# A second level of Strassen products for one more of the seven products in a tuned MLP kernel: four operand sums, results in tiles of their own, some differences on GpSimd

## The chip, the cores and the metric

The kernel runs on one core of one Trainium2 chip. The metric is device time in microseconds (us) for one execution; a lower time is better. The mean granted TensorE clock was 1.00 in the kernel before.

Names of engines as in the profile: PE is TensorE (matmuls), PEld its weight loads, DVE is VectorE, ACT is ScalarE, POOL is GpSimd, SP is the engine that issues most DMA loads (SPq is its sequencer).

## The reference

```python
x = randn(8, 1024, 1024); w1 = randn(1024, 4096); w2 = randn(4096, 1024)   # float32
h = x @ w1
h = 0.5 * h * (1 + tanh(sqrt(2 / pi) * (h + 0.044715 * h ** 3)))
return (h @ w2).astype(float32)
```

## The kernel before

The 8192 rows are handled as eight blocks of 1024 (0 to 7). In each block, M1 is `x @ w1` with the activation, and M2 is the product with `w2`. Both use Strassen's seven products instead of eight, with half-precision operands. In M2 some of those seven products are split once more, each into seven smaller ones (here called a *split* product; the others are *plain*). A plain product of M2 is 64 matmuls of 512 columns, a split one is 7 x 16 = 112 matmuls of 256 columns.

Blocks 0 and 1 make the weight sums and write them to DRAM (no split products). Block 2 splits products 6 and 7 and meanwhile makes the split weights of 1 and 3. Blocks 3 to 7, the *late blocks*, split 1, 3, 6 and 7. The order of products in M2 is 4, 1, 2, 3, 5, 6, 7.

One shared pool of 26 big tiles, `up` (4 KB in each of 128 partitions, shown as `u` in the profile), holds M1's weights, all weight tiles of M2, the operands made by VectorE, the next block's transposed x, and results on their way to DRAM.

```python
    up = ctx.enter_context(tc.tile_pool(name="up", bufs=26))
    gcp = ctx.enter_context(tc.tile_pool(name="gcp", bufs=4))      # operand sums, "gc"
    tp = ctx.enter_context(tc.tile_pool(name="tp", bufs=10))       # small temporaries, "tmp", 2 KB
    # ...
    class Inner:                                  # one split product
        def load(self):
            for j in ORDER:                       # seven weight tiles of 512 KB, issued by SP
                self.y[j] = unit(NI // 2, OH // 2)          # unit() takes a tile of `up`
                nc.sync.dma_start(out=self.y[j], in_=in_d[self.m][:, j - 1])
        def make_x(self, b): ...                  # one difference of g, VectorE, a tile of `up`
        def make(self, j): ...                    # one operand sum, VectorE, a tile of `gcp`; five per product
        def steps(self):
            # ...
            pb, qb, rb = psum(), psum(), psum()
            self.multiply(4, pb, True)            # 16 matmuls each
            v = temp()
            nc.scalar.copy(out=v, in_=pb)
            yield 4                               # fill-in work for VectorE stands at the yields
            self.multiply(5, qb, True)
            u = tile(results, 0)
            tt(u, v, qb, SUB, True)
            # ... 1, 2, 3, 7, 6: results go on in PSUM (pb, qb, rb), are added into acc,
            #     or leave through two result tiles
    # ...
    def matmul2(sb, g, next_x):
        # ...
        order = (4, 1, 2, 3, 5, 6, 7)
        load(4)
        run((0, 0))
        for m, after in zip(order, order[1:] + (None,)):
            if after is not None:
                load({1: 2, 2: 3, 3: 5}.get(m, after))     # loads of the next product
            if m == (1 if sb == 2 else 3):
                at["xs"] = next_x()               # 16 transposing loads, SP, four tiles of `up`
            if m in inner:
                for j in products[m].steps():
                    run((m, j))
                continue
            # ... a plain product; product 2 goes on in the PSUM banks of product 4
```

## Time and profile before

| | before |
|---|---|
| median of the first runs | 1542.41 us |
| PE busy | 1530.6 us of a span of 1541.5 |
| VectorE, ScalarE, GpSimd busy | 1072.1, 504.4, 278.1 us |
| DMA | 395.8 MB, mean 257 GB/s |

The head of the profile page, and its part 4, the chain of waits by engine:

```profile
PE 1530.6 (99%) x8318; PEld 814.8 (53%) x8318; DVE 1072.1 (70%) x1332; ACT 504.4 (33%) x852; POOL 278.1 (18%) x386
...
PE 94%; DMA 4%; DVE 1%; issue 0%; ACT 0%; SPq 0%; POOL 0%; DVEq 0%; POOLq 0%
```

The chain in order of time, for the M2 of block 4 and the M1 behind it. Columns: start (us), length (us), what; L757 are plain products, L675 split ones, L368 is M1:

```profile
884.97 13.81 PE ps L757 x64
898.79 12.23 PE ps L675 x112
911.01 13.81 PE ps L757 x64
924.83 12.23 PE ps L675 x112
937.05 13.81 PE ps L757 x64
950.87 24.45 PE ps L675 x224
975.32 96.69 PE ps L368 x448
```

There is no gap between the pieces: PE never waits here. A plain product takes 13.81 us and a split one 12.23 us, so splitting one more is worth 1.58 us.

SP's loads in the same M2, from its timeline (start, length of the run of issues, line, what, how many). The block's M2 starts at 884.97:

```profile
883.28 2.13 SPq L271 DMA_DIRECT2D u<-raw_d  x4
885.46 15.42 SPq L660 DMA_DIRECT2D u<-in_d  x7
904.06 3.81 SPq L271 DMA_DIRECT2D u<-raw_d  x4
908.05 21.92 SPq L352 DMA_TRANSPOSE u<-xb  x16
930.07 29.98 SPq L660 DMA_DIRECT2D u<-in_d  x14
```

These are the loads of products 2, 3, 5, the x of the next block, and products 6 and 7 (14 tiles). The first tile of product 6 is issued at 930, 21 us before PE needs it at 950.9. SP itself waits here for stores of results to land and free a tile, as its list of waits for this M2 shows:

```profile
SPq L660 <- DMA out_dram<-u: 20.7, 2, 13.2
```

PE does not feel these two waits, because the loads are still early enough.

### The profile page before, as it was taken

What the parts mean: (1) busy time and instruction counts of PE and PEld (TensorE: products, weight loads), DVE (VectorE), ACT (ScalarE), POOL (GpSimd) and SP (SyncE); (2) the same over time, 40 slices, a digit from 0 to 9 for tenths busy, and PEclk for the clock granted to TensorE, in tenths of its full rate; (3) what the DMA queues carried; (4) which work ended last, traced back from release to release, by engine and by line L of the source; (5) the groups of instructions that cost most, each with busy time, mean ns of one, the idle gap of its engine ahead of it and who ended that gap; (6) DMA issues with size and microseconds to landing.
All of it is one profiled execution on the core that took longest, in us unless ns stands there. A gap on an engine that the chain in (4) does not pass through costs nothing.

```text
span 1541.5 us, 22131 instructions
## 1 busy us (share of the span) xinstructions
PE 1530.6 (99%) x8318; PEld 814.8 (53%) x8318; DVE 1072.1 (70%) x1332; ACT 504.4 (33%) x852; POOL 278.1 (18%) x386
## 2 busy tenths in 40 slices
PE   9999999999999999999999999999999999999998
PEld 4444444444444447445664457544675447744466
DVE  5876867758755677557865578656786566955676
ACT  6655024410244112442134411344114431144311
POOL 1242011112201042001320013200141001400023
PEclk9999999999999999999999999999999999999999
DMA  9999875884985799957898589975799669994577
GB/s 310 346 329 348 250 272 188 282 254 148 349 271 161 195 369 315 310 150 236 259 321 291 135 251 293 331 234 175 221 315 326 193 182 257 304 342 131 187 251 192
DMA packets 211980, 395.76 MB, mean 257 GB/s; under 512 B 77344, under 2 KB 95776, under 8 KB 210976
## 3 DMA queue, kind: packets, MB, share of 16 engines
q1 hardware_dynamic: 175968, 297.86, 59.0%
q0 software_dynamic: 35904, 96.49, 23.0%
q8 instruction: 65, 1.06, 0.3%
q14 instruction: 43, 0.35, 0.1%
HBM read 294.65 MB, written 114.29 MB: 265 GB/s over the span
## 4 chain that ended last, share of the span: by engine, by line
PE 94%; DMA 4%; DVE 1%; issue 0%; ACT 0%; SPq 0%; POOL 0%; DVEq 0%; POOLq 0%
PE ps L368 49%; PE ps L757 29%; PE ps L675 16%; DMA u<-in_d 1%; DMA gc<-in_w_dram 1%; DMA u<-w_d 1%; DMA out_dram<-u 1%; DMA in_d<-u 1%; DVE u L150 0%; DVE tmp L150 0%; SPq L160 0%; ACT u L219 0%; POOL out_dram L466 0%; ACT g L378 0%; ACT u L323 0%
## 5 line engine op out<-in xcount | busy, mean ns | idle before, releaser
L368 PE MATMUL ps<-u 128*128 128x512 f16 x3584 | 776.3, 379 | 4.8 <-DVE tmp L150 1.9
L150 DVE TENSOR_TENSOR tmp<-tmp,ps 128x512 f32<-128x512 f32 x546 | 374.2, 687 | 309.2 <-ACT tmp L430 113.0
L368 PEld LDWEIGHTS <-u 128*128 128x128 f16 x3584 | 350.3, 98 | 428.5 <-issue 4.6
L757 PE MATMUL ps<-u,gc 128*128 128x512 f16 x1472 | 320.3, 379 | 0.0
L378 ACT ACTIVATE g<-tmp 128x512 f16<-128x512 f32 x256 | 161.2, 630 | 295.2 <-DVE tmp L150 295.1
L757 PEld LDWEIGHTS <-gc 128*128 128x128 f16 x1472 | 144.0, 98 | 171.6
L150 DVE TENSOR_TENSOR u<-u 128x2048 f16<-128x2048 f16 (+3 forms) x194 | 186.4, 989 | 28.6 <-ACT u L323 12.5
L675 PE MATMUL ps<-u,gc 128*128 128x256 f16 x1760 | 198.3, 273 | 0.0
L675 PEld LDWEIGHTS <-gc 128*128 128x128 f16 x1760 | 172.2, 98 | 19.9
L378 ACT ACTIVATE g<-ps 128x512 f16<-128x512 f32 x256 | 151.5, 596 | 89.8 <-PE ps L368 89.7
L757 PE MATMUL ps<-u,g 128*128 128x512 f16 x704 | 153.7, 379 | 0.0
L150 DVE TENSOR_TENSOR u<-u,ps 128x512 f32<-128x512 f32 x124 | 84.7, 683 | 51.9 <-PE ps L675 16.4
L150 DVE TENSOR_TENSOR gc<-g,g 128x2048 f16<-128x2048 f16 x92 | 113.8, 1244 | 3.0 <-PE ps L757 1.6
L757 PEld LDWEIGHTS <-g 128*128 128x128 f16 x704 | 68.9, 98 | 83.0
L474 POOL DMA_DIRECT2D out_dram<-u x84 | 81.9, 1105 | 132.7 <-ACT u L696 123.6
L150 DVE TENSOR_TENSOR gc<-u 128x2048 f16<-128x2048 f16 x85 | 102.3, 1219 | 0.0
L813 ACT COPY tmp<-ps 128x512 f32<-128x512 f32 x52 | 30.5, 586 | 196.2 <-PE ps L757 172.6
L150 DVE TENSOR_TENSOR tmp<-ps,tmp 128x512 f32<-128x512 f32 x128 | 88.4, 690 | 5.9 <-PE ps L368 1.2
L466 POOL DMA_DIRECT2D out_dram<-tmp x76 | 53.7, 712 | 212.0 <-ACT tmp L813 110.3
L430 ACT COPY tmp<-ps 128x512 f32<-128x512 f32 x128 | 72.9, 570 | 49.3 <-PE ps L368 36.0
L150 DVE TENSOR_TENSOR u<-g,g 128x2048 f16<-128x2048 f16 x68 | 80.2, 1220 | 3.5 <-ACT g L378 3.5
L713 POOL TENSOR_TENSOR u<-u,tmp 128x512 f32<-128x512 f32 x12 | 20.6, 1721 | 292.0 <-DVE tmp L150 288.3
(40 smaller groups left out, 501.1 us busy)
## 6 DMA issues: line engine op xcount, KB each, us to landing
u<-in_d SPq DMA_DIRECT2D x154, 512.0 KB, 6.2
u<-w_d SPq DMA_DIRECT2D x240, 256.0 KB, 5.4
u<-raw_d SPq DMA_DIRECT2D x80, 512.0 KB, 6.3
out_dram<-u POOLq DMA_DIRECT2D x116, 256.0 KB, 8.5
gc<-in_w_dram SPq DMA_DIRECT2D x48, 512.0 KB, 6.0
u<-raw_d SPq DMA_DIRECT2D x96, 256.0 KB, 5.7
out_dram<-tmp POOLq DMA_DIRECT2D x76, 256.0 KB, 5.5
raw_d<-u SPq DMA_DIRECT2D x32, 512.0 KB, 9.5
```

Source lines behind the costliest of these rows:

```text
L150: i = nc.vector.tensor_tensor(out=out, in0=in0, in1=in1, op=op)
L368: nc.tensor.matmul(bank, lhsT=ops[:, k, :], rhs=xs[m][:, k, :], start=(first and k == 0), stop=(k == KH - 1), skip_group_check=not first,)
L378: gelu_last[0] = nc.scalar.activation(out=g[b][:, c, :], in_=src, func=GELU)
L430: nc.scalar.copy(out=v, in_=pb)
L466: return nc.gpsimd.dma_start(out=out2[r0:r0 + P, o0:o0 + OH], in_=src, **kw)
L474: return queue.dma_start(out=rows, in_=src, **(dict(accum_op=ADD) if add else {}))
L675: nc.tensor.matmul(bank[:, i * OH // 2:(i + 1) * OH // 2], lhsT=t[:, c, i * P:(i + 1) * P], rhs=self.y[j][:, c, :], start=(first and i == ...
L713: nc.gpsimd.tensor_tensor(out=quarter(acc, b), in0=quarter(acc, b), in1=pair(t), op=ADD)
L757: nc.tensor.matmul(bank, lhsT=a[:, c, :], rhs=pieces[c // QC][:, c % QC, :], start=(first and c == 0), stop=(c == NI - 1), skip_group_chec ...
L813: nc.scalar.copy(out=t, in_=ps)
```

## The change

Its intent: split product 2 as well, so 28 split products instead of 22. To pay for the additional VectorE work, every split product uses a form with four operand sums on each side instead of five (four sums of g and four sums of weights), and gathers its four quarters in result tiles of its own; product 4's block is stored and product 2's quarters are added to it in DRAM. Half of the differences of g for products 1 and 2 are made by GpSimd during M1. The split weights of product 2 are made in block 1. Cut to its core:

```diff
-INNER = (6, 7, 1, 3)
-ORDER = (4, 5, 1, 2, 3, 7, 6)
+MADE_INNER = (6, 7)
+FROM_2 = (2,)
+INNER = MADE_INNER + FROM_2 + (1, 3)
+S_TERMS = {1: "11", 2: "12", 4: "22"}
+S_SUMS = {1: (5, "21", ADD, "22"), 2: (6, 1, SUB, "11"), 3: (7, "11", SUB, "21"), 4: (3, "12", SUB, 2)}
+EARLY = ((1, "11"), (1, "21"), (2, "11"), (2, "21"))
+W_ORDER = (1, 6, 2, 7, 5, 4, 3)
...
-    dict(inner=(1, 3, 6, 7), fill=fills(
-        s00="x122 x112 x111 x121 a15 a11 a12 a17", ...
+    dict(inner=(1, 2, 3, 6, 7), fill=slots("""00:x122 x112 a11 a12 a13 a14 x222 x212
+    ;12:a21;14:a22;15:a23;17:a24
+    ;21:u0 u1;22:a31;23:u2 u3;24:a32;25:a33 d11;26:d22;27:a34 d21 d12
+    ;32:g50;34:g51 e11;35:g52 e22;36:e21;37:g53 e12""" ...
-    dict(inner=(6, 7), ...                       # block 2
+    dict(inner=(2, 6, 7), ...
...
+            if sb > 1 and c >= NI - 4:            # M1, GpSimd
+                m, b = EARLY[c - NI + 4]
+                if m in FILL_2[sb == 2]["inner"]:
+                    early[m][b] = unit(NI // 2, HT // 2)
+                    gu, gv = (inner_block(g[t], b) for t in A_TERMS[m])
+                    nc.gpsimd.tensor_tensor(out=early[m][b], in0=gu, in1=gv, op=SUB)
...
+        def steps(self, into):                    # into: two tiles of `up`
+            ab, bb, cb = psum(), psum(), psum()
+            self.multiply(1, ab, True)
+            v = temp()
+            nc.scalar.copy(out=v, in_=ab)
+            yield 1
+            self.multiply(6, bb, True)
+            tt(c12, pair(v), pair(bb), ADD, True)
+            yield 2
+            self.multiply(2, ab, False)
+            nc.scalar.copy(out=c11, in_=pair(ab))
+            self.done("11", c11)
+            yield 3
+            self.multiply(7, bb, False)
+            tt(c21, pair(v), pair(bb), ADD, True)
+            # ... 5, 4, 3
...
         def post4(q, ps):
             nc.scalar.copy(out=u[q], in_=ps)
+            store(sb, "21", q, u[q])              # product 2's quarters are added to this in DRAM
...
-                load({1: 2, 2: 3, 3: 5}.get(m, after))
+                load(after)
```

The last two lines ask for the loads in the same order in both kernels; the change there is one of form.

## The prediction

> **What bounds the kernel now.** The matmul stream. PE has 94% of the chain of waits, which is almost one unbroken PE chain from 63 us to 1537.5 us; the list of waits has PE waiting under 8 us in all. The granted clock was 1.00. The time is start-up (some 60 us, untouched), the matmul pieces, and a 4 us tail.
>
> In the chain in order of time, a plain M2 product (64 matmuls of 512 columns) takes 13.81 us; one split at the second level (112 matmuls of 256 columns) takes 12.23 us; M1 takes 96.69 us per block. So weight loads (98 ns each) still hide behind a 109 ns half-width matmul, and a split is worth 1.58 us.
>
> **Removed, added, moved.**
> - PE: product 2 becomes split in all six late blocks. The other splits keep 112 matmuls in another order. 6 x 1.58 = 9.5 us less, all on the critical path. Matmuls of 256 columns go from 2464 to 3136.
> - VectorE, per late block: 128x2048 half-precision differences 45 -> 41 (1.22 us each, 1.14 us apart), 128x512 fp32 additions in M2 34 -> 41 (0.69 us, 0.60 us apart). About even: some 70 us of work in the 75 us after product 4. Counting VectorE by hand against PE, I find it 2 to 4 us behind after products 2 and 3, and nothing late for PE.
> - ScalarE: 24 -> 18 copies of 0.59 us. Not critical.
> - GpSimd: 12 fp32 additions (128x512, 1.27 to 2.18 us) go; 22 differences of 128x2048 come in the last four chunks of M1, by my estimate 4 x 1.27 = 5 us each. The Trainium skill ("SBUF - State Buffer", Who interferes with whom) says that a VectorE operation with two SBUF inputs and a GpSimd operation that reads SBUF block each other; the trace fits (beside a 2.18 us GpSimd addition a VectorE difference took 1.70 instead of 1.22 us). In M1 one VectorE input is PSUM, so only the last difference should collide with VectorE's first of M2. Hidden.
> - DMA: per late block 7 instead of 4 weight tiles of 0.5 MB (+1.6 MB), and product 4's "21" block is stored, then added to (+1 MB). DMA share is about 0.93 over M2, 1.0 to 1.1 in products 6, 7 and early M1, but 0.48 late in M1, and loads are issued two products ahead. This is the main risk: perhaps 5 to 9 us more DMA work per block, and 26 buffers cap the look-ahead. I expect 0 to 0.5 us of PE waiting per block.
> - Block 1 splits product 2's weights while VectorE idles 7.5 us in product 4: free.
>
> **Predicted.** 1542.4 - 9.5 + about 1.5 of new waits = 1534.5 us, 8 in 10 between 1530 and 1544. Faster by over 2%: 0.01; within 2%: 0.96; slower by over 2%: 0.03.
>
> **What would show it.** Right: late M2 sections in the chain of 88.8 us instead of 90.4; PE idle under 10 us in the list of waits; VectorE busy within 1% of 1072 us; GpSimd busy up by 70 to 100 us; DMA moving 20 to 25 MB more. Wrong: PE waiting for weight tiles of products 2, 3 or 6, or for VectorE in products 3 or 6.
>
> **What would make it wrong.** Loads starved of buffers (the four early tiles hold them during M1), adding stores holding up the GpSimd queue and thereby buffers, or VectorE lagging over 5 us, which stalls PE on a PSUM bank.

## More of the kernel before

All runs that are compared here are of the fast state.

Part 6 of the page, the group of split weights (kilobytes each, median us from issue to landing):

```profile
u<-in_d SPq DMA_DIRECT2D x154, 512.0 KB, 6.2
```

## The result, and the profile after

The changed kernel takes 1579.24 us (median of 4 runs), the kernel before 1543.62 us in the same rounds: ratio 1.023, with a 95% interval of 1.0206 to 1.0253. It is correct and slower. Ratios here are the mean time of one kernel's fast runs over that of the other's fast runs of the same rounds, so they are not quite the ratio of the medians quoted.

The same views of the changed kernel. The head of the page and the chain of waits by engine:

```profile
PE 1531.9 (97%) x8606; PEld 839.5 (53%) x8606; DVE 1066.9 (68%) x1354; ACT 486.2 (31%) x821; POOL 387.2 (25%) x434
...
PE 75%; DMA 14%; DVE 4%; issue 4%; SPq 1%; ACT 1%; POOL 1%; POOLq 0%; DVEq 0%
```

PE has 75% of the chain instead of 94%. PE's list of waits (engine, line, what it waited for: us in total, times, longest), first the longest entry before, then the top of the list after:

```profile
PE ps L368 <- DVE tmp L150: 1.9, 2, 1.4
```

```profile
PE ps L686 <- DVE u L146: 11.9, 5, 10.3
PE ps L686 <- DMA u<-in_d: 11.8, 11, 2.0
PE ps L686 <- ACT tmp L704: 4.3, 6, 0.7
PE ps L686 <- DVE gc L146: 3.3, 6, 1.4
PE ps L364 <- DMA u<-w_d: 3.3, 9, 0.5
```

SP's timeline in block 4; M2 starts at 901.67 here:

```profile
887.19 35.80 SPq L668 DMA_DIRECT2D u<-in_d  x21
929.00 3.95 SPq L267 DMA_DIRECT2D u<-raw_d  x4
933.12 26.81 SPq L348 DMA_TRANSPOSE u<-xb  x16
960.03 18.34 SPq L668 DMA_DIRECT2D u<-in_d  x14
```

The loads of products 6 and 7 start at 960.0, which is 58 us into M2 instead of 45, and only 8 us before PE needs the first of them at 968.06. PE's timeline there, with the waits in brackets:

```profile
971.56 1.91 PE L686 MATMUL ps<-u 128*128 128x256 f16 x16
975.42 1.92 PE L686 MATMUL ps<-u,gc 128*128 128x256 f16 x16 [1.96 <-DMA u<-in_d]
978.04 1.38 PE L686 MATMUL ps<-u 128*128 128x256 f16 x11 [0.70 <-DMA u<-in_d]
...
991.99 3.65 PE L686 MATMUL ps<-u,gc 128*128 128x256 f16 x32 [1.07 <-DMA u<-in_d]
```

The loads also take longer from issue to landing, by part 6 of the page (6.2 us before):

```profile
u<-in_d SPq DMA_DIRECT2D x196, 512.0 KB, 7.8
```

From the landing times in the traces, counted after 700 us: mean 6.2 and 90th percentile 9.1 us before, 8.8 and 17.3 us after.

Block 2 shows a second kind of wait. VectorE's timeline, then PE's:

```profile
595.85 2.36 DVE L146 TENSOR_TENSOR u<-g,g 128x2048 f16<-128x2048 f16 x2 [11.15 <-DMA out_dram<-u]
```

```profile
598.27 3.53 PE L686 MATMUL ps<-u 128*128 128x256 f16 x16 [10.29 <-DVE u L146]
```

VectorE waits 11.15 us to write a new difference into a tile, because a store of results out of that tile has not landed. These differences are PE's own operand: the second of them ends at 598.21 and PE's matmuls start at 598.27, after waiting 10.29 us. (With 28 tiles, in experiment 12, it is the emptying of PSUM, queued on VectorE behind such a difference, that PE waits for.)

**Where the time went.** To add it up I took, from each trace, the distance between the starts of successive matmuls less the regular spacing (215.8 ns for 512 columns, 109.2 ns for 256), and summed what was over 60 ns. In us, one profiled run each:

```
              M2 of block 2   M2 of blocks 3-7   M1 of blocks 3-7
before              0.7              0.0                1.0
after              16.5             27.3                6.0
```

The change lost 49.8 us of PE time from block 2 on where before lost 1.7. That is 48 us of new waiting against the 9.5 us gained; with some 1 us less in the start-up it agrees with the measured difference of the two spans, 1578.6 - 1541.5 = 37.1 us.

**A third thing in the trace: the order of PE's work.** The order of instructions in the built programs (it is fixed when the kernel is compiled) shows that the scheduler moved PE's matmul groups. In block 3, written with the product (1, 2) and the part:

```
program order:  1.1 1.6 1.2 1.7 1.5 1.4 1.3 | 2.1 2.6 2.2 2.7 2.5 2.4 2.3
emitted, after: 1.1 1.6 1.2 1.5 2.1 2.2 1.4(2) 1.7 1.4(14) 2.6(6) 1.3 2.6(10) 2.5 ...   (n): n of 16 matmuls
```

Part 2.2 stands straight behind 2.1 and adds to the same PSUM bank, which ScalarE must copy first: those are the waits for `ACT tmp L704`. It should also hold the weight tiles of two products for longer; that was not measured.

### The profile page after: what moved, and what is told of

It reads as the page before. It is cut to its first block, busy times and chain, and to the rows that moved or that the text cites. A ratio compares the mean times of both kernels' runs of the same rounds, so it can differ in the third digit from the quotient of the medians.

```text
span 1578.6 us, 22771 instructions
## 1 busy us (share of the span) xinstructions
PE 1531.9 (97%) x8606; PEld 839.5 (53%) x8606; DVE 1066.9 (68%) x1354; ACT 486.2 (31%) x821; POOL 387.2 (25%) x434
## 4 chain that ended last, share of the span: by engine, by line
PE 75%; DMA 14%; DVE 4%; issue 4%; SPq 1%; ACT 1%; POOL 1%; POOLq 0%; DVEq 0%
PE ps L364 46%; PE ps L749 20%; PE ps L686 9%; DMA u<-in_d 6%; DMA u<-w_d 3%; DMA out_dram<-u 3%; DVE u L146 3%; DMA gc<-in_w_dram 2%; DVE gc L146 1%; DMA in_d<-u 1%; SPq L156 1%; DMA out_dram<-tmp 1%; ACT u L803 0%; SPq L348 0%; POOL u L159 0%
## 5 line engine op out<-in xcount | busy, mean ns | idle before, releaser
L364 PEld LDWEIGHTS <-u 128*128 128x128 f16 x3584 | 349.1, 98 | 433.8 <-DMA u<-w_d 8.5
L749 PE MATMUL ps<-u,gc 128*128 128x512 f16 x1088 | 237.4, 380 | 0.0
L146 DVE TENSOR_TENSOR u<-u 128x2048 f16<-128x2048 f16 (+3 forms) x245 | 219.0, 923 | 18.2 <-ACT u L319 12.2
L686 PEld LDWEIGHTS <-gc 128*128 128x128 f16 x1792 | 174.1, 98 | 36.8 <-issue 9.0
L749 PEld LDWEIGHTS <-gc 128*128 128x128 f16 x1088 | 106.4, 98 | 126.3
L477 POOL DMA_DIRECT2D out_dram<-u x108 | 111.5, 1033 | 246.6 <-DVE u L146 183.2
L460 POOL TENSOR_TENSOR u<-g,g 128x2048 f16<-128x2048 f16 x22 | 89.1, 4072 | 296.9 <-ACT g L374 296.9
L686 PE MATMUL ps<-u 128*128 128x256 f16 x1104 | 136.4, 275 | 23.4 <-DVE u L146 11.2
L686 PEld LDWEIGHTS <-u 128*128 128x128 f16 x1104 | 107.8, 98 | 43.8 <-DVE u L146 17.0
L146 DVE TENSOR_TENSOR u<-tmp,ps 128x512 f32<-128x512 f32 x56 | 38.4, 686 | 109.4 <-PE ps L686 72.0
L146 DVE TENSOR_TENSOR u<-g,g 128x2048 f16<-128x2048 f16 x70 | 83.5, 1220 | 19.6 <-DMA out_dram<-u 11.1
L427 ACT COPY tmp<-ps 128x512 f32<-128x512 f32 x128 | 72.9, 569 | 73.8 <-PE ps L364 73.6
L146 DVE TENSOR_TENSOR gc<-g,g 128x2048 f16<-128x2048 f16 x68 | 82.3, 1219 | 3.0 <-PE ps L749 1.6
```

The costliest lines, as they stand in the source:

```text
L146: i = nc.vector.tensor_tensor(out=out, in0=in0, in1=in1, op=op)
L364: nc.tensor.matmul(bank, lhsT=ops[:, k, :], rhs=xs[m][:, k, :], start=(first and k == 0), stop=(k == KH - 1), skip_group_check=not first,)
L460: nc.gpsimd.tensor_tensor(out=early[m][b], in0=gu, in1=gv, op=SUB)
L477: return queue.dma_start(out=rows, in_=src, **(dict(accum_op=ADD) if add else {}))
L686: nc.tensor.matmul(bank[:, i * OH // 2:(i + 1) * OH // 2], lhsT=t[:, c, i * P:(i + 1) * P], rhs=self.y[j][:, c, :], start=(first and i == ...
L749: nc.tensor.matmul(bank, lhsT=a[:, c, :], rhs=pieces[c // QC][:, c % QC, :], start=(first and c == 0), stop=(c == NI - 1), skip_group_chec ...
```

## The experiments

Theories at the outset. **O**: the interleaved PE order is the cause, directly and by holding tiles. **S**: 26 tiles and the DMA traffic do not suffice for five split products, in whatever order; I came to divide this into *tiles* and *bytes*. **F**: the four-sum form with its own results costs by itself. Each edit below is against the changed kernel unless it says otherwise. "Lost" is PE time lost as in the table above, in the order M2 of block 2 / M2 of blocks 3 to 7 / M1 of blocks 3 to 7.

Two cautions. The ratio is to the kernel before in the same rounds; times of different experiments are medians from different rounds, in which the kernel before took 1540.8 to 1543.0 us (1543.6 beside the changed kernel), so up to 3 us of a difference need not come from the edit. And every edit is a new build in which tiles are handed out anew, which was not held fixed: experiment 12, 27 us above experiment 5, shows what that can cost, so a difference of a few us between two builds is weak evidence.

### 1. PE in program order

```diff
-                    nc.tensor.matmul(                 # in multiply() and matmuls2()
+                    tc.keep_in_program_order(nc.tensor.matmul(
```

> Only change to the changed kernel: every M2 matmul is pinned in program order on PE. The emitted order of the changed kernel takes up the first matmul groups of the next split product before the last ones of the present one, wherever two split products follow each other. Theory O (this interleaving is the cause: waits inside PE, and weight tiles of two products held at once, so later loads): 1535 to 1548 us, late M2 sections back at 89 to 90 us. Rival S (26 buffers and the added DMA traffic are too little for five split products in any order): stays above 1565 us, PE still waiting for in_d loads. Rival F (the four-sum form itself costs): no change, about 1579.

1570.8 us, ratio 1.019. Lost 12.2 / 7.7 / 21.7. Most of M2's waits in the late blocks went, and M1's waits grew from 6.0 to 21.7: a wait removed in one place came back in the next. PE's list of waits now has on top:

```profile
PE ps L364 <- DMA u<-w_d: 11.0, 10, 2.9
PE ps L686 <- DVE u L146: 9.0, 8, 4.1
```

The load that M1 waits for could not be issued. SP's timeline, with its M1 loads (L254) at the end of block 4's M2, and SP's list of waits in the stretch between them:

```profile
981.41 0.32 SPq L254 DMA_DIRECT2D u<-raw_d  x1
991.97 1.82 SPq L254 DMA_DIRECT2D u<-w_d  x4
```

```profile
SPq L254 <- DMA out_dram<-u: 10.1, 1, 10.1
```

SP waited 10.1 us for a result store to land, because that store frees the tile into which the weights go. The kernel before has the same kind of wait at this place, and the same four loads (from SP's list of waits and its timeline):

```profile
SPq L258 <- DMA out_dram<-u: 7.7, 1, 7.7
964.87 9.42 SPq L258 DMA_DIRECT2D u<-w_d  x4
```

There they begin 10.5 us before M1 does (at 975.32), here 0.6 us after it (at 991.37). So the wait for the store is not new; the slack that hid it is gone. O is at most a part; the tiles come free too late.

### 2. The form alone

Product 2 stays plain (22 split products), all else as in the change:

```diff
-FROM_2 = (2,)
+FROM_2 = ()
-    dict(inner=(1, 2, 3, 6, 7), ...      # and inner=(2, 6, 7) -> (6, 7) in block 2
+    dict(inner=(1, 3, 6, 7), ...
+        def post2(q, ps):
+            c = copy(q, ps)
+            store(sb, "21", q, c, accum_op=ADD)
+            tt(u[q], u[q], rows[1][q], ADD, True)
+            tt(rows[1][q], rows[1][q], c, SUB, True)
```

> Four-sum form and own results everywhere, half of product 1's differences on GpSimd, but product 2 stays plain as before (so 22 split products, not 28). Theory F (form costs): 1565 us or more. Theories O and S (the cost comes with product 2's split): 1541 to 1552 us, PE waits small.

1548.25 us, ratio 1.0046 (1.0031 to 1.0061). Lost 3.2 / 4.3 / 0.0. The form, results and GpSimd differences without the split of product 2 cost some 7 us: F is a small part. PE's list of waits has no load among its entries.

### 3. No early differences on GpSimd

```diff
-            if sb > 1 and c >= NI - 4:
+            if False:
-    ... 00:x122 x112 a11 a12 a13 a14 x222 x212
+    ... 00:x122 x112 x111 x121 a11 a12 a13 a14 x222 x212 x211 x221
```

> The changed kernel with all differences for products 1 and 2 on VectorE at the head of M2, none on GpSimd in M1. If the four tiles that GpSimd's differences hold during M1, or its work, starve the loads: at least 10 us less than 1579. If VectorE needs the help: 5 to 20 us more. Theory O: within 8 us of 1579, as the PE order stays as interleaved.

1577.84 us, ratio 1.024. Lost 15.5 / 28.7 / 5.8, as in the changed kernel. Neither GpSimd's work nor the four early tiles, as long as the rest is unchanged, make the difference. (In the changed kernel's trace GpSimd makes these differences from 857 to 874 us, 27 us and more before M2 at 901.67; the scheduler moved them ahead of where the program has them.)

### 4. One tile more

```diff
-    up = ... bufs=26        tp = ... bufs=10
+    up = ... bufs=27        tp = ... bufs=8
```

> The changed kernel with 27 instead of 26 big buffers, paid for with two of the ten small temporaries (no more fits). Theory S (buffers): 5 to 15 us less than 1579. Theory O: within 4 us of 1579.

1567.74 us, ratio 1.0174. Lost 14.1 / 17.4 / 3.8. One tile in 26 is worth 11.5 us (8.7 if each kernel is taken against the kernel before of its own rounds), as the tile theory expected. More does not fit beside ten temporaries.

### 5. Program order and 27 tiles

> The changed kernel with both: PE in program order, and 27 big buffers (8 small temporaries). If order and buffers are two parts of one cause (weight tiles loaded too late because tiles come free too late), the two gains (8 and 11 us) add up or more: 1545 to 1560 us, and the waits for w_d at the head of M1 shrink. If the limit is DMA bandwidth, the tile more helps no further: 1565 us or more.

1554.12 us, ratio 1.008. Lost 9.3 / 3.0 / 8.6. The two gains add up to more than their sum (25 against 8 + 11.5, or 22.5 against 5.6 + 8.7 with each against its own rounds), as they should if order and tiles act on one limit.

### 6. Program order and less store traffic

Product 4's block is not stored and added to; VectorE adds it to product 2's results (the kernel has that path already, as `base`).

```diff
-            2: Inner(2, g, lambda b, t: store_quarter(sb, "21", b, t), x=early[2]),
+            2: Inner(2, g, lambda b, t: store_quarter(sb, "21", b, t, add=False), u2, x=early[2]),
-            store(sb, "21", q, u[q])                 # in post4
```

> Program order on PE, and product 4's block is no longer stored and then added to in memory: VectorE adds it to product 2's results (right result, 1 MB written and 1 MB of adding stores less per block, the same number of tiles). Bandwidth theory: 8 us or more under the 1570.8 of the run with program order alone. Buffer theory: within 5 us of it, or up to 8 us less if landing times of the stores, which free the result tiles, get shorter.

1575.16 us, ratio 1.0213: slower than experiment 1, not faster. Lost 14.9 / 14.3 / 11.4. M1's waits fell by 10 us, but my edit put eight VectorE additions in a bunch at the end of product 2, and PE waited 2.85 us for VectorE in each late block. The total did not fall, but the edit was not clean, so this run does not settle what the bytes of the stores cost.

### 7. Program order, product 2 plain in block 2

In block 2 product 2 is plain, and its weights are split there instead of in block 1.

> Program order on PE, and in block 2 alone (the one that also splits weights) product 2 stays plain, 27 split products in all. Block 2's M2 lost 12.2 us in the run with program order alone, waiting for VectorE, which waits for a tile that an adding store frees. If that comes with product 2's split, 1558 to 1562 us; if it comes with the form or with writing the split weights later, 1568 us or more.

1575.03 us, ratio 1.0214. Lost 14.9 / 5.2 / 21.7. My edit moved two things at once: it took the split of product 2 out of block 2 and put the splitting of its weights into it. So this run does not tell whether block 2's waits come from product 2 being split there. Experiment 18 leaves the weights' splitting in block 1 with product 2 plain in block 2, and loses 4.8 us in block 2 where experiment 5 loses 9.3 (it also shortens M1's look-ahead). Experiments 2 and 10, where product 2 is never split, lose 3. So the split of product 2 in block 2 seems to be part of it; the rest was not taken apart.

### 8. The kernel before with 25 tiles

```diff
-    up = ctx.enter_context(tc.tile_pool(name="up", bufs=26))    # the kernel before
+    up = ctx.enter_context(tc.tile_pool(name="up", bufs=25))
```

> The kernel before with 25 instead of 26 big buffers, nothing else. Buffer theory: before was already near the edge, so 3 to 15 us slower than before. Bandwidth theory: within 2 us of before.

1554.5 us, ratio 1.0083: one tile less costs the old kernel 13.5 us. Lost 1.6 / 0.0 / 10.0. PE's wait is of the same kind as in experiment 1:

```profile
PE ps L368 <- DMA u<-w_d: 6.6, 7, 1.6
```

So the kernel before stood at the edge: it had the tiles it needed and none to spare. PE's list of waits does not show that; SP's does, with its 20.7 us until stores landed.

### 9. Program order and half the bytes of all split weights (wrong result)

```diff
-                nc.sync.dma_start(out=self.y[j], in_=in_d[self.m][:, j - 1])
+                nc.sync.dma_start(out=self.y[j][:, :NI // 4, :], in_=in_d[self.m][:, j - 1, :NI // 4, :])
-                        rhs=self.y[j][:, c, :],
+                        rhs=self.y[j][:, c % (NI // 4), :],
```

> Wrong result on purpose: the run with program order on PE, but each tile of split weights is loaded with half its bytes (the matmuls use the loaded half twice). Same tiles, same number of loads, same PE work; 9 MB of some 50 MB less per late block. Bandwidth theory: nearly all waits go, 1530 to 1540 us. Buffer theory: the loads still cannot start before a tile is free, so 1558 us or more.

1533.35 us, ratio 0.9947. Lost 0.3 / 1.6 / 0.0. With the same tiles and the same PE work, nearly everything that was waited for is there in time, and most of the gain on PE appears: 9.5 us were predicted, and this is 7.8 us under the kernel before. The edit takes away more than the change added: 363.8 MB are moved, against 415.2 in the changed kernel and 395.8 before. So it shows what faster loads do, and not that the added bytes were the cause (for that see experiment 17). My expectation for tiles alone (1558 or more) was wrong. Part 6 of its page:

```profile
u<-in_d SPq DMA_DIRECT2D x196, 256.0 KB, 4.5
```

The loads land in 4.5 us, and result stores land sooner as well (group `out_dram<-u` from POOL: median 6.2 instead of 8.2 us), so tiles come free sooner. A number of tiles that sets the time whatever the loads take is refuted here; bytes that set it whatever the number of tiles are refuted by experiments 4 and 5. The reading that fits both is that what counts is how many tiles there are and how fast each is filled, used and emptied.

### 10. The form alone, in program order

> The form alone (product 2 plain, as in the run of the form) with PE in program order. Theory: the 0.83 us that the form lost per late block was interleaving too, so 1539 to 1546 us. If instead pinning itself costs (block 2's wait for VectorE got no better with it), 1550 us or more.

1546.15 us, ratio 1.0026. Lost 2.9 / 1.9 / 0.0. About half of what the form lost in late blocks was the order. The rest, some 5 us, is mainly block 2 (2.9) and 0.4 us per late block.

### 11. Program order, 27 tiles, the x of the next block loaded later

```diff
-            if m == (1 if sb == 2 else 3):
+            if m == (1 if sb == 2 else 5):
                 nxt[0] = next_x()
```

> Program order, 27 big buffers, and the 16 transposing loads of the next block's x (4 tiles, held until M1's end) issued one product later, behind the loads of product 6. Buffer theory: four tiles less for some 12 us in the tightest place, and the loads of 6 no longer wait behind transposes: 1538 to 1550 us, under the 1554 of the run with 27. If the queue's total is the limit: 1554 us or more.

1576.01 us, ratio 1.0236: 22 us worse than experiment 5. Lost 11.9 / 38.5 / 5.1, in a profiled run that was the slowest of the four (1587.6 us; the others took 1574 to 1577). Four tiles are asked for later, but in block 4 the transposing loads then stand between those of products 6 and 7 (issued from 942.66 to 976.44), and PE waits 5.76 us there for a load of product 7. In the whole run its waits for VectorE are 24.5 us. A miss for the tile theory in its simple form.

### 12. Program order and 28 tiles

Six temporaries instead of ten.

> Program order and 28 big buffers, paid for with four of ten small temporaries. Buffer theory: M1's waits for w_d go from 2 us to under 0.5 us per block, and the total to 1538 to 1550 us, unless six temporaries are too few for M1, which would show as waits for ScalarE or VectorE on tmp in M1.

1580.93 us, ratio 1.0249. Lost 12.4 / 36.0 / 0.0. M1's waits for loads are gone, as expected, but there is a new one in M2. VectorE's timeline in block 4:

```profile
966.73 1.22 DVE L146 TENSOR_TENSOR gc<-u,gc 128x2048 f16<-128x2048 f16 x1
975.56 1.23 DVE L146 TENSOR_TENSOR u<-g,g 128x2048 f16<-128x2048 f16 x1 [7.61 <-DMA out_dram<-u]
```

It is block 2's wait again: the tile for a difference is one whose result store has not landed, and PE then waits 7.9 us for VectorE. Which tile follows which is fixed when the kernel is compiled; with another number of tiles, another operation meets the late store. A tile more is no sure gain when the holder in front of it is a slow store. (The temporaries went from ten to six as well; the waits named here are for tiles of `up`, and M1 lost nothing, but their share was not tested by itself.)

### 13 and 14. Less store traffic with VectorE's additions spread, 26 and 27 tiles

As 6, with the additions distributed over products 2 and 3.

> As the run with program order and less traffic (product 4's block added on VectorE to product 2's results, nothing stored and added to later), but VectorE's additions are spread over products 2 and 3; there they stood in a bunch at the end of product 2 and cost 2.85 us of PE waiting per late block. If traffic counts, M1's waits for w_d stay at 2 to 3 us per block as there and the bunch's cost goes: 1553 to 1563 us. If not: 1568 us or more.

> The same with 27 big buffers (8 small temporaries). If tiles and bytes are two factors of one limit: 1538 to 1552 us, below the 1554 of order and 27 buffers. If tile turnover is set by something else: 1554 us or more.

1575.89 us (1.022) and 1563.54 us (1.0137). Lost 14.0 / 10.6 / 19.6 and 13.5 / 8.7 / 5.9. Both are 5 to 9 us slower than the same without the edit (experiments 1 and 5), so taking away 6 MB of stores in all did not pay: product 2's result tiles are then held into product 3, and VectorE has more to do. The tile more is again worth 12 us, here in the same rounds.

### 15. Half the bytes alone (wrong result)

> Wrong result on purpose: the changed kernel with its own interleaved PE order and half the bytes in each load of split weights. Tells what the order costs when loads are never late: the waits for ScalarE and VectorE that the interleaving brings are some 2 us per late block in the changed kernel's trace, so 1540 to 1549 us against 1533 with program order. If order costs nothing by itself: within 3 us of 1533.

1534.58 us, ratio 0.9955. Lost 0.4 / 2.5 / 0.0. My expectation rested on an order that stays interleaved, and it did not: counted in the traces as stretches of successive matmuls of one line and one kind of operands, there are 223 against 246 in the changed kernel and 215 in program order (experiment 9). With smaller loads the scheduler interleaves less, which suggests that it interleaved because it reckoned the loads late. So the order in the changed kernel may be mostly a consequence of the load problem, and this run does not tell what the order costs by itself.

### 16. As 14, with two differences of product 2 made later

> The run with order, less traffic and 27 buffers, and the two of product 2's differences that VectorE makes are made in product 1 instead of product 4, so two tiles are held some 14 us less. Tile theory: 1 to 6 us below that run, and 1534 to 1548 us. Otherwise no change or slower.

1560.2 us, ratio 1.0117. Lost 14.6 / 9.0 / 6.7. It is 3.3 us better than 14 by the medians and far from the kernel before.

### 17. Program order, half the bytes of product 2's weights alone (wrong result)

> Wrong result on purpose: program order on PE, and only product 2's split weights are loaded with half their bytes, so that a late block loads no more bytes than before (1.8 MB for product 2 instead of 3.7 MB; before 2.1 MB), with the changed kernel's number of tiles. Bytes that the split added as the cause: 1531 to 1545 us. Tiles held as the cause: 1558 us or more. Both as factors of one limit: between.

1566.06 us, ratio 1.0154: only 4.7 us better than experiment 1 (6.9 with each against its own rounds). Lost 9.5 / 7.0 / 16.1. This kernel loads no more weight bytes in a late block than the kernel before, and still loses most of the time. So the weight bytes that the split adds are a small part. By elimination the larger part is what it adds in tiles and in the time that they are held; no run isolates it. The wait is where experiment 1 has it:

```profile
PE ps L364 <- DMA u<-w_d: 9.8, 12, 2.1
```

### 18. A try for a version under both kernels

Program order, 27 tiles, product 2 plain in block 2 (its weights split in block 1), and a shorter look-ahead in the second half of M1:

```diff
-                    ... min(c // 2 + 3, NI // 2)
+                    ... min(c // 2 + (3 if c < 8 else 2), NI // 2)
```

> A try for a correct version under both kernels: program order, 27 big buffers, product 2 plain in block 2 only (its weights still split in block 1), and in M1 from chunk 8 on the weight look-ahead is two half-quads instead of three, so that two or three tiles come free for M2's first loads in M1's idle DMA time. From the 1554 of order and 27 buffers: block 2 gives back 5 us, the earlier loads up to 8 us in M1's waits for w_d and the slower M1: 1536 to 1550 us. If look-ahead in M1 matters, M1 itself will show waits for w_d late in it.

1549.52 us, ratio 1.0038 (1.0016 to 1.0060). Lost 4.8 / 3.6 / 8.0. It is the best correct version with product 2 split, 30 us under the changed kernel, and still slower than the kernel before. No correct kernel of this study beats the kernel before.

## Why the prediction was wrong, point by point

- *The gain on PE, 6 x 1.58 = 9.5 us.* Right. With loads that are never late (experiment 9) late M2 sections take 89.1 us where 88.8 was predicted and 90.35 was measured before; the time was 1533.35 us, where 1534.5 was predicted for the real kernel.
- *VectorE about even, ScalarE less, GpSimd 70 to 100 us more.* VectorE's busy time is 1066.9 us against 1072.1, within 1% as predicted; GpSimd's rose by 109 us, over the range: the 22 differences took 89 us (4.07 us each, I had estimated 5), the 12 additions that went had taken 21, and most of the rest is longer issuing of DMAs, which I had left out (the stores from `u` to `out_dram`: 120 us before, 152 after). The Trainium skill ("GPSIMD Engine Reference", Elementwise - side-by-side cycle accounting) gives 4.5 us for an addition of this length in fp32; here it is a difference in half precision and took 4.07 us. The collision of GpSimd with VectorE that I feared from "SBUF - State Buffer" did not come up, as GpSimd was done at 874 us, before VectorE's first two-SBUF operation at 903 (block 4); beyond the 1.70 us in the prediction no run here tests it.
- *DMA, 20 to 25 MB more.* It is 19.4 MB (415.2 against 395.8), just under the range.
- *"I expect 0 to 0.5 us of PE waiting per block."* **This is the step that failed**, by its size. The mechanism that the prediction named as the main risk, 26 buffers that cap the look-ahead, was the right one; I set its cost at 1.5 us in all and it was 48 us: 16 in block 2 and some 6 to 7 us per late block with its M1. I had looked at the DMA's share as if idle DMA time late in M1 (0.48) could be used. Loads need a free tile, not only a free queue. The kernel before has no tile to spare (experiment 8: one less costs 13.5 us), and the split needs three more weight tiles, two more result tiles and up to four tiles of differences for product 2.
- *Loads issued two products ahead.* True before (21 us ahead for product 6). After, they were 8 us ahead, with a landing time that rose from 6.2 to 7.8 us (median of the whole run) and from 9.1 to 17.3 us (90th percentile after 700 us).
- *"About even ... nothing late for PE" from VectorE.* Wrong in block 2, where VectorE waits up to 11.15 us for a store to free its output tile. PE waits there for the difference itself. I had counted VectorE's work and not what its outputs wait for.
- *The order of matmul groups.* Not foreseen: I took the emitted order for the program's. Experiment 15 suggests that the scheduler interleaves because it reckons loads late. Pinning the order gave 8 us, mostly by moving waits into M1.

What is shown: more tiles help (4, 5, 14; with the exception of 12, where the new wait is named), fewer hurt (8), faster loads of all split weights remove nearly all waits (9, 15), and fewer bytes for product 2 alone remove few of them (17). What stays open: which of the added holders of tiles (weights, results or differences) counts how much, what the interleaved order costs by itself, and what makes block 2 lose so much (experiment 7 changed two things at once).

## What to carry to other kernels

Before adding work that loads or holds more, test how close to the edge the kernel is: take one buffer away from the old kernel. Look also at what the loads themselves wait for (`--waits --engine SP`): in the old kernel they already waited up to 13.2 us for a store to free a tile, while PE waited for nothing. If the buffer taken away costs more than the change is to gain, the change must bring its own buffers, however idle DMA looks on average. When a wait is removed and the time hardly moves, compare where PE waits in both traces, since a limit on tile turnover shows up now as a late load, now as an operand's producer waiting for its output tile, and a new buffer count can move it to a worse place.

## What the Trainium skill lacked or had wrong

- "DMA: Bandwidth & Descriptors", Anatomy of one DMA, gives a fit for one DMA that GpSimd issues of about 2.0 us plus bytes / 436 GB/s, so 3.2 us for 512 KB (an estimate from the page). GpSimd's own 512 KB stores took 4.5 us (`w_d<-u`) and 6.6 us (`in_d<-u`) before, 4.3 and 8.2 after, by the medians. The fit is not given for loads that SP issues; here these took 6.2 us before, and 7.8 us with 17.3 us at the 90th percentile after. I found no word there that such landing times set how fast buffers come free.
- The same page, Latency and other measured facts, gives 261 GB/s for transposing DMA with a non-contiguous middle dimension, and more where it is contiguous. In the changed kernel's stretch from 940.1 to 955.8 us, which the transposing loads dominate but do not have to themselves, all DMA moved 158 GB/s. Why it is that far below was not taken apart by a run.
- "TensorE: Matmul & The Clock Gate", What's actually happening, says that the clock falls after an idle window of about 3.4 us. This is no lack: the trace agrees, though no run here measures the length of that window. In block 2's 10.3 us wait the granted clock was 0.66, and the next 16 matmuls of 256 columns took 3.53 us instead of 1.91, so that wait cost 1.6 us more than its length.
- No page that I read says that a VectorE result can wait for the landing of a store that last used its tile (11.15 us in block 2, 7.61 us with 28 tiles), or puts a size on one buffer: here one big tile of 26 was worth some 9 to 13.5 us (experiments 4 and 8), and a 28th made things worse.
